# The gate ahead of the mixer by row blocks, twelve pairs of weight halves held, the norm's row folded into the scale

## The chip, the core and the metric

The kernel runs on one core of one Trainium2 chip. Its engines work side by side and wait for each other by semaphores: TensorE (PE in the rows) multiplies matrices and transposes, VectorE (DVE) does element-wise work, ScalarE (ACT) evaluates functions and copies, GpSimd (POOL) does some element-wise work, and SyncE (SP) issues the weight loads. Each engine takes its instructions in the order in which they stand in its queue. The metric is the time of one execution on the device in microseconds, of which the median over several runs counts.

## What is computed

The reference is a large block (a linear recurrence, attention, a mixture of 64 experts, a gate) followed by a second one (a mixer with window attention and a convolution). The change lies at the joint of the two:

```python
    ple_gate = jax.nn.sigmoid(rmsnorm(x, ln_ple[layer]) @ w_ple_gate[layer])
    x = x + (p[layer] @ w_ple_proj[layer]) * ple_gate
    return x
...
    sh, sc, gt = _modulation(c, w_mod[i], b_mod[i])
...
    h = _rmsnorm(x, pre_g[i]) * (1.0 + sc[:, None, :]) + sh[:, None, :]
...
    parts = _split_in(h @ w_in[i])
```

There are 256 rows (tokens) and 1024 columns. The gate is a 1024 by 1024 matrix multiplication, a sigmoid (made from a tanh) and a sum into `x`. Then `x` is normed by row, scaled by a row vector, shifted by another, and multiplied by `w_in_2` (10,240 columns).

## The kernel before

A row block `i` is 128 rows, and there are two; a column chunk `c` is 512 columns, and the gate has two. `x`, `acc` (the sum so far), `pp` (`p @ w_ple_proj`) and `x3g` (the normed `x`) lie with rows on the partitions. A matrix multiplication needs its left side with columns on the partitions, so `x3g` is transposed on TensorE, four 128x128 pieces into a PSUM bank (`transpose4`), and taken out of the bank as two halves, `hi` and `lo` (`hl_from_bank`): ScalarE writes `hi`, VectorE subtracts it for `lo`. The result, `h2`, holds 8 row groups `kt` of 128 columns, two halves and 256 tokens. Weights are halved in the same way (`split`): ScalarE casts `hi` and VectorE or GpSimd subtracts for `lo` (`sub_turn`: "v" is VectorE always, "vg" the two in turn). Each product is then three matmuls, 512 columns wide: hi by hi, lo by hi, hi by lo. Pairs of weight halves live in pools of four pairs: `spp`, `sp`, `sx`; `Held` gives two more. A pair's buffer comes free when its last matmul is done.

In the kernel before, the gate's chunk 0 goes through `gemm_nat` (both row blocks for each `kt`, 48 matmuls) and chunk 1 through `gemm_rows` (row block 0 over all eight `kt`, then row block 1). `take_gate` finishes each of the four blocks: tanh, two VectorE steps, the square sum of the norm, and for three of them the multiplication by the scale row (`mixer_gain`). `mixer_scale(i)` closes a block's norm, with the power on GpSimd (`rstd`), and multiplies by the norm's factor and adds the shift row. `mixer_columns(i)` transposes the block. Chunk 2 of `w_in_2` follows by `gemm_rows`: row block 0, the transposes of block 1, row block 1. `post_row` makes a row vector that is needed much later, with two matmuls in fp32. `row_of` made three such rows in the expert stage (expert group 13), among them the scale row and the shift row (`rows2`).

Then come chunks 3, 0, 1, 4 and 5 of `w_in_2` by `gemm_nat` (`qkv_lane`), with the pairs from `sp` alone and the subtractions by VectorE and GpSimd in turn. Woven into chunk 3 are the transposes of the keys of chunk 2 (`k_lane`, `stack_heads`): `take_rope` turns each block of chunk 2 with three kinds of VectorE steps into `kx`, `hi_lo` makes the two halves `kn` of it (a cast on ScalarE, a subtraction on GpSimd), and TensorE transposes these. `kx` has one buffer.

The order on each queue comes from a scheduler that takes what the code lists and estimates when things are ready; TensorE alone stands in the order of the code. `tc.issue_after` adds that one instruction stands behind another on the same engine.

## Time and profile before

| | us |
|---|---|
| median of 3 runs | 1130.07 |
| the three runs | 1130.07, 1131.84, 1127.13 |
| the profiled execution | 1129.72 |
| its span, first to last instruction | 1128.1 |
| TensorE busy in the span | 1031.7 (91%) |
| VectorE, ScalarE, GpSimd busy | 572.7, 424.3, 300.3 |

The span is what the trace shows; 1.6 us lie around it. The joint, from the gate's first matmul to the first matmul of chunk 3 of `w_in_2`, runs from 735.1 to 780.5 us of the span. In a timeline row the first number is the start, the second the length, and a bracket gives how long the engine stood idle before it and what ended that. Neighbouring matmuls overlap, so their pace is read from their starts and not from their lengths.

### The profile page before, as it was taken

How to read it: one execution, taken by the hardware profiler on the slowest of the kernel's cores; microseconds unless marked ns; L12 is line 12 of the kernel's file. 1: busy time of each engine (PE TensorE's matmuls, PEld its weight loads, DVE VectorE, ACT ScalarE, POOL GpSimd, SP SyncE). 2: the span in 40 equal slices, each digit the busy share in tenths (PEclk: the TensorE clock that was granted, in tenths of full speed). 3: DMA queues.
4: the chain of work that ended last, by engine and by line, in shares of the span. 5: the costliest groups of instructions: out<-in, count | busy, mean ns of one | idle time of the engine just before them, and what ended most of it. 6: DMA issues, size and time to landing. Idle time of an engine off the chain costs nothing.

```text
span 1128.1 us, 17631 instructions
## 1 busy us (share of the span) xinstructions
PE 1031.7 (91%) x6844; PEld 730.8 (65%) x6848; DVE 572.7 (51%) x1155; ACT 424.3 (38%) x875; POOL 300.3 (27%) x257
## 2 busy tenths in 40 slices
PE   8998899999999769999996788798999999999997
PEld 6886679985444134444442233176889989999996
DVE  6967896474333122321222232186847798752465
ACT  6766754550111030100110011164457646545553
POOL 2554474450000000000000000003553363554462
PEclk9998999999999889999999798899999999999999
DMA  8672468778999999999999999972554434345531
GB/s 348 250 281 78 158 244 291 302 279 318 419 421 419 422 419 420 421 421 422 421 421 419 420 422 420 420 285 75 187 201 164 141 128 139 127 155 184 185 113 38
DMA packets 47260, 321.49 MB, mean 285 GB/s; under 512 B 5762, under 2 KB 6274, under 8 KB 9411
## 3 DMA queue, kind: packets, MB, share of 16 engines
q1 hardware_dynamic: 47090, 320.04, 72.3%
q8 instruction: 56, 0.92, 0.3%
q14 instruction: 34, 0.27, 0.1%
q0 software_dynamic: 80, 0.26, 0.1%
HBM read 319.23 MB, written 1.05 MB: 284 GB/s over the span
## 4 chain that ended last, share of the span: by engine, by line
PE 63%; DMA 19%; DVE 11%; ACT 3%; issue 3%; POOL 1%; SPq 0%; DVEq 0%; POOLq 0%; ACTq 0%
DMA w<-in_w_dram 19%; PE mm L246 8%; PE mm L248 8%; PE mm L247 8%; PE mm L1256 5%; PE mm L1296 3%; PE mm L209 3%; PE mm L208 3%; PE mm L210 3%; PE ps L1239 3%; PE ps L1223 3%; PE mm L1130 2%; PE mm L970 2%; DVE lo L191 2%; PE ps L173 2%
## 5 line engine op out<-in xcount | busy, mean ns | idle before, releaser
L187 ACT CAST hi<-w 128x512 fp32r<-128x512 f32 (+2 forms) x340 | 205.6, 617 | 178.9 <-PE mm L247 125.5
L191 POOL TENSOR_TENSOR lo<-w,hi 128x512 fp32r<-128x512 f32 x144 | 198.3, 1379 | 229.3 <-ACT hi L187 221.4
L191 DVE TENSOR_TENSOR lo<-w,hi 128x512 fp32r<-128x512 f32 (+2 forms) x196 | 148.3, 766 | 115.5 <-ACT hi L187 105.6
L1256 PE MATMUL mm<-w,xe 128*32 128x512 f32 x1024 | 128.8, 640 | 29.8 <-DMA w<-in_w_dram 22.7
L246 PE MATMUL mm<-h,hi 128*128 128x256 f32 x448 | 129.5, 289 | 0.0
L248 PE MATMUL mm<-h,lo 128*128 128x256 f32 x448 | 126.7, 283 | 0.1
L247 PE MATMUL mm<-h,hi 128*128 128x256 f32 x448 | 126.6, 283 | 0.0
L1256 PEld LDWEIGHTS mm<-w,xe 128*32 128x32 f32 x1024 | 30.2, 114 | 115.8 <-issue 60.8
L1278 DVE SCALAR_TENSOR_TENSOR th<-th,mm 128x256 f32<-128x256 f32 x16 | 6.7, 421 | 180.3 <-ACT th L1277 180.3
L246 PEld LDWEIGHTS mm<-h,hi 128*128 128x128 f32 x448 | 85.6, 191 | 3.1 <-issue 3.1
L248 PEld LDWEIGHTS mm<-h,lo 128*128 128x128 f32 x448 | 85.7, 191 | 0.3 <-DVE lo L191 0.3
L247 PEld LDWEIGHTS mm<-h,hi 128*128 128x128 f32 x448 | 85.7, 191 | 0.0
L1296 PE MATMUL mm<-w,hE 128*32 128x512 f32 x512 | 64.3, 626 | 15.9 <-DMA w<-in_w_dram 11.4
L1277 ACT ACTIVATE th<-mm 128x256 f32<-128x256 f32 x16 | 6.1, 384 | 192.1 <-PE mm L1256 175.5
L1241 DVE TENSOR_TENSOR acc<-acc,ps 128x512 f32<-128x512 f32 x60 | 41.2, 687 | 65.3 <-PE ps L1239 65.2
L1351 POOL DMA_DIRECT2D tabs<-in_tabs_dram x1 | 0.7, 737 | 269.5 <-DMA w<-in_w_dram 269.5
L1223 PEld LDWEIGHTS ps<-G,x 128*128 128x128 f32 x512 | 60.9, 198 | 15.2 <-issue 13.5
L1239 PE MATMUL ps<-y,cT 128*128 128x512 f32 x128 | 61.6, 624 | 9.8 <-ACT y L1302 9.8
L248 PE MATMUL mm<-hT,lo 128*128 128x256 f32 x224 | 65.1, 291 | 2.6 <-DVE lo L191 2.6
L169 POOL TENSOR_TENSOR s<-s,half 128x1 f32<-128x1 f32 (+1 forms) x6 | 4.0, 668 | 237.4 <-DVE s L167 237.4
L246 PE MATMUL mm<-hT,hi 128*128 128x256 f32 x224 | 66.5, 297 | 0.0
L247 PE MATMUL mm<-hT,hi 128*128 128x256 f32 x224 | 64.7, 289 | 0.0
(474 smaller groups left out, 2145.2 us busy)
## 6 DMA issues: line engine op xcount, KB each, us to landing
w<-in_w_dram SPq DMA_DIRECT2D x192, 1024.0 KB, 19.8
w<-in_w_in_dram SPq DMA_DIRECT2D x66, 1024.0 KB, 5.0
w<-in_w_mod_dram SPq DMA_DIRECT2D x12, 1024.0 KB, 8.2
w<-in_w_out_dram SPq DMA_DIRECT2D x4, 1024.0 KB, 7.9
w<-in_w_ple_gate_dram SPq DMA_DIRECT2D x4, 1024.0 KB, 12.3
w<-in_w_out_conv_dram SPq DMA_DIRECT2D x4, 1024.0 KB, 4.7
w<-in_w_out_attn_dram SPq DMA_DIRECT2D x4, 1024.0 KB, 4.7
w<-in_w_o_dram SPq DMA_DIRECT2D x4, 1024.0 KB, 4.8
```

Source lines behind the costliest of these rows:

```text
L187: nc.scalar.copy(hi[:, :n], wt[:, off:off + n])
L191: last_sub[eng is G] = eng.tensor_sub(lo[:, :n], wt[:, off:off + n], hi[:, :n])
L208: mm(ps[m][:, :n], ah, wh, start=kt == 0, stop=False)
L209: mm(ps[m][:, :n], al, wh, start=False, stop=False)
L246: mm(o, hi[:, c:c + P], ah, start=kt == 0 and b % 2 == 0, stop=False)
L247: mm(o, hi[:, c:c + P], al, start=False, stop=False)
L248: mm(o, lo[:, c:c + P], ah, start=False, stop=kt == kts - 1 and b % 2 == 1)
L1223: mm(b[:, k * P:(k + 1) * P], x[:, i, kt * P:(kt + 1) * P], Gt[i].rearrange("p e s -> p (e s)"), start=i == 0, stop=i == 1)
L1239: mm(b, cT[:, i * P:(i + 1) * P], y[:, c * 512:(c + 1) * 512], start=True, stop=True)
L1241: V.tensor_add(acc[:, i, s_], (acc if q else x)[:, i, s_], b)
L1256: mm(ps[32 * j:32 * j + 32, :], xe[:, kt, 32 * j:32 * j + 32], wt[:, j * 512:(j + 1) * 512], start=kt == 0, stop=kt == KT - 1)
L1296: mm(ps[32 * j:32 * j + 32, :], hE[:, ft, 32 * j:32 * j + 32], wt[:, j * 512:(j + 1) * 512], start=ft == 0, stop=ft == 1)
```

## The change

The gate's two chunks go through one new function, `gemm_turns`. It multiplies row block 0 by both chunks first (with the first four `kt` of chunk 0 for row block 1 as well), holds the other twelve pairs of weight halves in `sp`, `sx` and `spp`, and multiplies row block 1 by them afterwards. `take_gate` is cut in two, the tanh and the rest (`gated`). The multiplication by the scale row is folded into `mixer_scale` (one instruction: `x` by the norm's factor by the scale row), so `mixer_gain` goes, and the row of the shift is no longer made in the expert stage. The shift is added instead where the transposed block leaves PSUM: there it is one number for each partition, and each of the eight 128x128 pieces of a block has a column of its own, so a block leaves in eight ScalarE and eight VectorE steps of 128 columns instead of two and two of 512. The halves of `w_in_2`'s chunk 2 (`halve`, two `kt` at a time) are put by hand between these steps, the transposes of row block 0 stand between the gate's last matmuls, and `post_row` moves behind the transposes of row block 1.

```diff
+    def gemm_turns(sps, actT, chunks, done):
...
+        for c in range(2):
+            for kt in range(KT):
+                hl[c, kt] = split(sps[c * 2 + kt // 4], wt[c][kt // 4], (kt % 4) * 512, 512)
+                terms(c, 0, kt)
+                if c == 0 and kt < 4:
+                    terms(c, 1, kt)
+                if kt % 2:
+                    yield
+        for c in range(2):
+            done(c, 0, ps[c, 0])
+        for c in range(2):
+            for kt in range(4 - 4 * c, KT):
+                terms(c, 1, kt)
+                if kt % 2:
+                    yield
+            done(c, 1, ps[c, 1])
...
-            row_of(gd, rows2[:, 0], gpre)
-            row_of(gd, rows2[:, 1], modT)
+            row_of(gd, rows2, gpre)
...
-            chain_[i].append(V.scalar_tensor_tensor(x3g[:, i, s_], x3g[:, i, s_], r, rows2[:, 1, s_],
-                                                    op0=ALU.mult, op1=ALU.add))
+            done = V.scalar_tensor_tensor(x3g[:, i, s_], x[:, i, s_], r, rows2[:, s_], op0=ALU.mult, op1=ALU.mult)
...
-            turned = hl_from_bank(h2, c * 4, i, b)
+            with then(*turned):
+                turned = []
+                for j in range(4):
+                    kt = c * 4 + j
+                    src, shift = b[:, j * P:(j + 1) * P], modT[:, kt, 0:1]
+                    hi = act(h2[:, kt, 0, t_], src, AF.Identity, bias=shift)
+                    lo = V.scalar_tensor_tensor(h2[:, kt, 1, t_], src, shift, h2[:, kt, 0, t_], op0=ALU.add, op1=ALU.subtract)
+                    turned = [hi, lo]
...
-    lane = gemm_nat(spp, pT, chunk("w_ple_gate", 0), 512, both(take_gate(0)))
+    lane = gemm_turns((spp, sp, sx, spp), pT, [chunk("w_ple_gate", c) for c in range(2)], take_gate)
...
+    def halve(kt):
+        hl2[kt] = split((ahead, sp, sx, spp)[kt // 2], wt2[kt // 4], (kt % 4) * 512, 512)
...
+    weave((some(lane, 3), 1))
+    with then(scaled, chain_[0]):
+        halve(2)
+        halve(3)
+    with then(last_sub[False]):
+        second = gated(0, 1)
     turned = mixer_columns(0)
...
+    weave((lane, 1))
+    with then(turned[1]):
+        halve(4)
+        halve(5)
+    with then(last_sub[False]):
+        third = gated(1, 1)
+    with then(third, chain_[1]):
+        halve(6)
+        halve(7)
+    with then(last_sub[False]):
         mixer_scale(1)
```

What this does to the queues stands at three places. First TensorE, where the transposes of row block 0 stand (`pT` is the gate's left side, `mm_6152` and `mm_5962` the bank of chunk 1, row block 1, L1414 is `post_row`, `mm_6209` and `mm_6237` chunk 2 of `w_in_2`). Before:

```order
L227 MATMUL mm_6152<-hi_6135,pT_5789 128x512
L228 MATMUL mm_6152<-lo_6136,pT_5789 128x512
L1414 MATMUL ps_6185<-gtp_6181,ones_84 128x512
L1414 MATMUL ps_6188<-gtp_6181,ones_84 128x512
L173 MATMUL ps_6191<-cst_68,x3g_5965 128x128 x4
L173 MATMUL ps_6198<-cst_68,x3g_5965 128x128 x4
L226 MATMUL mm_6209<-ahead_6184,h2_5962 128x512
```

And now:

```order
L267 MATMUL mm_5962<-lo_6079,pT_5781 128x512
L173 MATMUL ps_6174<-cst_68,x3g_5957 128x128 x4
L173 MATMUL ps_6187<-cst_68,x3g_5957 128x128 x4
L265 MATMUL mm_5962<-hi_6085,pT_5781 128x512
L266 MATMUL mm_5962<-hi_6085,pT_5781 128x512
L267 MATMUL mm_5962<-lo_6086,pT_5781 128x512
```

The transposes of row block 0 moved ahead of the gate's last twelve matmuls, which now stand between them and the first use of their result, and `post_row` no longer stands there.

Second VectorE, from the transposed block 0 on, with the engines that each instruction waits for (`h2` is the transposed block, `lo_6255` and `lo_6262`, now `lo_6225` and `lo_6229`, are the `lo` halves of the last two `kt` of chunk 2's weights). Before:

```order
L1361 SCALAR_TENSOR_TENSOR x_69<-tq_5781,acc_3211 128x512 [waits DVE_49]
L179 TENSOR_TENSOR h2_5962<-ps_6191,h2_5962 128x4x128 [waits Activation_49]
L179 TENSOR_TENSOR h2_5962<-ps_6198,h2_5962 128x4x128 [waits Activation_49]
L1369 TENSOR_TENSOR x3g_5965<-x_69,rows2_5620 128x512 [waits DVE_49]
L1373 TENSOR_TENSOR s3_5966<-s3_5966 128x1 [waits Activation_49]
L191 TENSOR_TENSOR lo_6255<-w_6207,hi_6254 128x512 [waits Activation_49]
L167 TENSOR_SCALAR s3_5966<-s3_5966 128x1 [waits DVE_49]
L191 TENSOR_TENSOR lo_6262<-w_6207,hi_6261 128x512 [waits Activation_49]
```

And now, from the last four pieces of the block on:

```order
L1427 SCALAR_TENSOR_TENSOR h2_5954<-ps_6187,modT_80,h2_5954 128x128 [waits Activation_49] x3
L191 TENSOR_TENSOR lo_6214<-w_6133,hi_6213 128x512 [waits DMAHW1_49]
L191 TENSOR_TENSOR lo_6218<-w_6133,hi_6217 128x512
L1394 SCALAR_TENSOR_TENSOR tq_5773<-tq_5773,pp_4813 128x512
L1395 SCALAR_TENSOR_TENSOR x_69<-tq_5773,acc_3211 128x512 [waits DVE_49]
L191 TENSOR_TENSOR lo_6225<-w_6133,hi_6224 128x512 [waits PE_49,Activation_49]
L191 TENSOR_TENSOR lo_6229<-w_6133,hi_6228 128x512 [waits PE_49,Activation_49]
```

The weight halves of the last four `kt` of chunk 2 now stand behind all eight pieces of block 0, and the last two of them also behind the gate's last block. On ScalarE, which makes `hi` of each piece (L1426), the same place reads so now (L1389 is a tanh, L1396 a square):

```order
L1426 ACTIVATE h2_5954<-ps_6174,modT_80 128x128 [waits PE_49]
L1426 ACTIVATE h2_5954<-ps_6174,modT_80 128x128 [waits DVE_49]
L1396 ACTIVATE tq_5773,s3_5958<-x_69 128x512 [waits DVE_49]
L1426 ACTIVATE h2_5954<-ps_6174,modT_80 128x128 [waits DVE_49]
L1389 ACTIVATE tq_5773<-mm_5962,s1_2578 128x512 [waits PE_49]
L1426 ACTIVATE h2_5954<-ps_6174,modT_80 128x128 [waits DVE_49]
L1426 ACTIVATE h2_5954<-ps_6187,modT_80 128x128
L1426 ACTIVATE h2_5954<-ps_6187,modT_80 128x128 [waits DVE_49] x3
L1396 ACTIVATE tq_5773,s3_5958<-x_69 128x512 [waits DVE_49]
L187 CAST hi_6224<-w_6133 128x512 [waits Activation_49]
```

Where two casts of 512 columns waited for TensorE alone before, each piece but the first of a bank now waits for VectorE, with a square and a tanh in between, and the cast for `kt` 6 stands behind the square of the gate's last block.

Third ScalarE in chunk 3, by name (`hi_6393`, `hi_6403` are the casts of `kt` 2 and 3 before, `hi_6405`, `hi_6415` now; `kn_6303` and `kn_6315` are the first keys, `kn_6339` and `kn_6351` the second). Before:

```order
L187 CAST hi_6393<-w_6359 128x512
L978 CAST kn_6303<-kx_6295 128x8x64
L187 CAST hi_6403<-w_6359 128x512
L187 CAST hi_6427<-w_6425 128x512
L187 CAST hi_6437<-w_6425 128x512
L978 CAST kn_6339<-kx_6331 128x8x64
L187 CAST hi_6447<-w_6425 128x512
L187 CAST hi_6457<-w_6425 128x512
```

And now:

```order
L187 CAST hi_6405<-w_6371 128x512
L187 CAST hi_6415<-w_6371 128x512
L187 CAST hi_6439<-w_6437 128x512
L1011 CAST kn_6315<-kx_6307 128x8x64
L187 CAST hi_6449<-w_6437 128x512
L187 CAST hi_6459<-w_6437 128x512
L187 CAST hi_6469<-w_6437 128x512
L1011 CAST kn_6351<-kx_6343 128x8x64
```

The cast of the first keys moved behind those of `kt` 3 and 4, that of the second keys behind those of `kt` 6 and 7. GpSimd follows. Before:

```order
L191 TENSOR_TENSOR lo_6372<-w_6359,hi_6371 128x512
L979 TENSOR_TENSOR kn_6303<-kx_6295,kn_6303 128x8x64
L191 TENSOR_TENSOR lo_6404<-w_6359,hi_6403 128x512
L191 TENSOR_TENSOR lo_6438<-w_6425,hi_6437 128x512
L979 TENSOR_TENSOR kn_6339<-kx_6331,kn_6339 128x8x64
L191 TENSOR_TENSOR lo_6458<-w_6425,hi_6457 128x512
```

And now:

```order
L191 TENSOR_TENSOR lo_6384<-w_6371,hi_6383 128x512
L191 TENSOR_TENSOR lo_6416<-w_6371,hi_6415 128x512
L1012 TENSOR_TENSOR kn_6315<-kx_6307,kn_6315 128x8x64
L191 TENSOR_TENSOR lo_6450<-w_6437,hi_6449 128x512
L191 TENSOR_TENSOR lo_6470<-w_6437,hi_6469 128x512
L1012 TENSOR_TENSOR kn_6351<-kx_6343,kn_6351 128x8x64
```

The first keys' subtraction moved behind that of `kt` 3, the second keys' behind that of `kt` 7.

## Rows read from the trace of the kernel before

**Rows 1.** The page: busy us, share of the span and instructions of each engine.

```profile
PE 1031.7 (91%) x6844; PEld 730.8 (65%) x6848; DVE 572.7 (51%) x1155; ACT 424.3 (38%) x875; POOL 300.3 (27%) x257
```

**Rows 2.** Windows, sum of 783 to 1128 us: length, busy time by engine.

```profile
sum 345.00, PE 334.95 PEld 311.26 DVE 225.37 ACT 181.90 POOL 165.56; mean PE 47.85 PEld 44.47 DVE 32.20 ACT 25.98 POOL 23.65
```

**Rows 3.** Timeline of TensorE from 735 to 781 us: start, length, operation, idle before.

```profile
735.09 0.80 PE L208 MATMUL mm<-hi,pT 128*128 128x512 f32 x1
...
739.53 0.48 PE L208 MATMUL mm<-hi,pT 128*128 128x512 f32 x1
...
745.65 0.50 PE L208 MATMUL mm<-hi,pT 128*128 128x512 f32 x1 [0.41 <-ACT hi L187]
...
751.56 0.39 PE L226 MATMUL mm<-hi,pT 128*128 128x512 f32 x1
...
759.88 1.88 PE L1414 MATMUL ps<-gtp,ones 128*128 128x512 f32 x4
763.70 1.29 PE L173 MATMUL ps<-cst,x3g 128*128 128x128 f32 x8 [1.94 <-DVE x3g L1377]
...
766.20 0.79 PE L227 MATMUL mm<-ahead,h 128*128 128x512 f32 x1 [0.70 <-DVE h L179]
...
773.10 1.03 PE L173 MATMUL ps<-cst,x3g 128*128 128x128 f32 x8
774.37 0.49 PE L226 MATMUL mm<-ahead,h 128*128 128x512 f32 x1 [0.24 <-ACT h L179]
...
780.49 0.40 PE L208 MATMUL mm<-hi,h 128*128 128x512 f32 x1
```

**Rows 4.** Windows of 1 us, with PEclk, the granted clock, after the five engines.

```profile
767.00:768.00 1.00, 1.00 (x3) 0.79 (x3) 1.00 (x5) 0.33 (x1) 0.00 (x0) 0.50 0.06 16
...
769.00:770.00 1.00, 1.00 (x5) 0.82 (x4) 0.88 (x2) 0.00 (x0) 0.09 (x1) 0.77 0.54 66
```

**Rows 5.** Timeline of TensorE in the expert stage, around the rows of `row_of` (L1195).

```profile
671.71 5.83 PE L1195 MATMUL ps<-gd,ones 128*128 128x512 f32 x12
...
683.03 1.06 PE L1256 MATMUL mm<-w,xe 128*32 128x512 f32 x8 [1.07 <-DMA w<-in_w_dram]
```

**Rows 6.** Timeline of VectorE at the joint.

```profile
746.67 5.51 DVE L191 TENSOR_TENSOR lo<-w,hi 128x512 fp32r<-128x512 f32 x9 [0.35 <-ACT hi L187]
...
760.31 0.69 DVE L1361 SCALAR_TENSOR_TENSOR x<-tq,acc 128x512 f32<-128x512 f32 x1
...
762.80 1.41 DVE L1377 SCALAR_TENSOR_TENSOR x3g<-x3g,s,rows 128x512 f32<-128x512 f32 x2 [0.67 <-POOL s L169]
```

**Rows 7.** Timeline of ScalarE at the joint.

```profile
740.29 6.35 ACT L187 CAST hi<-w 128x512 fp32r<-128x512 f32 x12
...
761.03 0.63 ACT L1362 ACTIVATE tq<-x 128x512 f32<-128x512 f32 x1 [1.48 <-DVE x L1361]
```

**Rows 8.** Groups by shape on ScalarE: count, busy us, mean ns of one, idle before.

```profile
L779 ACT ACTIVATE on<-ob 128x128 f32<-128x128 f32 x8 | 2.1, 270 | 0.7 <-PE ob L774 0.7
L450 ACT ACTIVATE cf<-ps,vec 128x128 f32<-128x128 f32 x6 | 1.7, 376 | 0.0
```

**Rows 9.** The same on VectorE.

```profile
L1460 DVE TENSOR_TENSOR rot<-mm,tabs 128x128 f32<-128x128 f32 x32 | 7.0, 276 | 0.0
L783 DVE SCALAR_TENSOR_TENSOR on<-ob,r,og 128x128 f32<-128x128 f32 x8 | 2.4, 346 | 2.1 <-POOL r L169 2.1
```

**Rows 10.** Timeline of ScalarE in chunk 3.

```profile
783.88 0.62 ACT L978 CAST kn<-kx 128x512 fp32r<-128x512 f32 x1
785.36 0.62 ACT L187 CAST hi<-w 128x512 fp32r<-128x512 f32 x1 [0.86 <-PE mm L209]
```

**Rows 11.** Timeline of GpSimd in chunk 3.

```profile
783.98 1.29 POOL L191 TENSOR_TENSOR lo<-w,hi 128x512 fp32r<-128x512 f32 x1 [1.65 <-ACT hi L187]
785.23 1.29 POOL L979 TENSOR_TENSOR kn<-kx,kn 128x512 fp32r<-128x512 f32 x1
```

**Rows 12.** Timeline of TensorE in chunk 3, the transposes of the second keys.

```profile
786.70 0.80 PE L985 MATMUL ps<-identr,kn 128*128 128x128 f32 x8
```

More of the change, by code (lines that the diff above doesn't have):

```diff
@@ L213, in gemm_nat, with gemm_rows @@
                 yield
-    def gemm_rows(sps, actT, halves, n, done):
-        wt = [wload(src, 4 * n) for src in halves]
-        hl = {}
+    def gemm_rows(sps, actT, halves, n, done, hl=None):
+        given = hl is not None
+        if not given:
+            wt = [wload(src, 4 * n) for src in halves]
+            hl = {}
         for m in range(NT):
@@ L220, in gemm_rows @@
             for kt in range(KT):
-                if m == 0:
+                if m == 0 and not given:
                     hl[kt] = split(sps[kt % len(sps)], wt[kt // 4], (kt % 4) * n, n)
@@ L251, in gemm_t, with terms @@
                 yield
+    def gemm_turns(sps, actT, chunks, done):
+        ps = {(c, m): bank("mm") for c in range(2) for m in range(NT)}
+        wt = [[wload(src) for src in halves] for halves in chunks]
+        hl = {}
+        def terms(c, m, kt):
+            wh, wl = hl[c, kt]
+            ah = actT[:, kt, 0, m * P:(m + 1) * P]
+            al = actT[:, kt, 1, m * P:(m + 1) * P]
+            mm(ps[c, m], ah, wh, start=kt == 0, stop=False)
+            mm(ps[c, m], al, wh, start=False, stop=False)
+            mm(ps[c, m], ah, wl, start=False, stop=kt == KT - 1)
+        for c in range(2):
[14 more added lines that the diff above has]
+            done(c, 1, ps[c, 1])
     class Held:
@@ L1317 @@
             gple = gd[:, :D]
[L1318 removed]
+            rows2 = md.tile([P, D], F32, name="rows2", tag="fT")
             row_of(gd, gple, vcol("ln_ple")[:, :, None])
[L1320 to L1321 removed]
+            row_of(gd, rows2, gpre)
         if q == NQ - 2:
@@ L1376, in mixer_scale, with then @@
             s_ = slice(c * 512, (c + 1) * 512)
-            chain_[i].append(V.scalar_tensor_tensor(x3g[:, i, s_], x3g[:, i, s_], r, rows2[:, 1, s_],
-                                                    op0=ALU.mult, op1=ALU.add))
+            done = V.scalar_tensor_tensor(x3g[:, i, s_], x[:, i, s_], r, rows2[:, s_], op0=ALU.mult, op1=ALU.mult)
+        return done
+    def then(*made):
+        order = ExitStack()
+        for m in made:
+            order.enter_context(tc.issue_after(m.ins))
+        return order
     def mixer_columns(i):
+        t_ = slice(i * P, (i + 1) * P)
+        turned = []
         for c in range(2):
@@ L1397 @@
     weave((some(lane, 1), 1))
-    chain_ = {}
     with tc.issue_after(seen[0].ins), tc.issue_after(seen[1].ins):
-        weave((lane, 1))
-        with tc.issue_after(last_sub[False].ins):
-            lane = gemm_rows((sp, sx), pT, chunk("w_ple_gate", 1), 512, take_gate(1))
-            weave((some(lane, 4), 1))
-        mixer_scale(0)
-        with tc.issue_after(chain_[0][0].ins), tc.issue_after(chain_[0][-1].ins):
-            weave((lane, 1))
-    dump("x3", x)
+        weave((some(lane, 7), 1))
+    with tc.issue_after(last_sub[False].ins), tc.issue_after(tanhs[1, 0].ins):
+        gated(0, 0)
+        first = gated(1, 0)
     gtp = ha.tile([P, D], F32, name="gtp")
@@ L1420 @@
                         modT[:, 16 + 4 * c:20 + 4 * c, 0:1].to_broadcast([P, 4, P]), op=ALU.mult)
[L1421 removed]
+    held, hl2 = {}, {}
     ahead = Held(w0.tile([P, 4, 512], F32R, name="ahead", tag="w"))
[L1423 to L1430 removed]
+    wt2 = [wload(src) for src in chunk("w_in_2", 2)]
+    def halve(kt):
+        hl2[kt] = split((ahead, sp, sx, spp)[kt // 2], wt2[kt // 4], (kt % 4) * 512, 512)
+    with then(first, tanhs[0, 0]):
+        halve(0)
+        halve(1)
+    with then(last_sub[False]):
+        scaled = mixer_scale(0)
+    weave((some(lane, 3), 1))
[4 more added lines that the diff above has]
+        second = gated(0, 1)
+    turned = mixer_columns(0)
+    weave((lane, 1))
[7 more added lines that the diff above has]
+        halve(7)
+    with then(last_sub[False]):
         mixer_scale(1)
[L1432 to L1433 removed]
+    dump("x3", x)
+    lane = gemm_rows(None, h2, None, 512, held.__setitem__, hl2)
+    weave((some(lane, 4), 1))
     turned = mixer_columns(1)
+    post_row(0)
+    post_row(1)
     spp_cm.__exit__(None, None, None)
```

32 lines of the change are left out of this document (9 added, 23 removed).

## The prediction

> **What bounds the kernel now.** I read the page first, then the windows, then one timeline per engine at the joint. TensorE is busy for 91% of the span [rows 1]. Behind the joint it is busy for 334.95 of 345.00 us [rows 2]: what TensorE loses or wins up to 783 us comes out at the end unchanged, and only TensorE's queue has to be followed. Around the joint it is another matter. From the gate's first matmul at 735.09 to the first of chunk 3 at 780.49 are 45.4 us [rows 3]. The pace of the wide matmuls is 36 from 751.56 to 759.88, 0.231 us each. The work of the stretch is 96 + 48 of these (33.3), three sets of eight transposes at 1.03 (3.1) and the post rows (1.9): 38.3 us. So 7.1 us are to be had there at most. They are seen in rows 3: a wait of 1.94 for VectorE's `x3g`, one of 0.70 for `h`, and smaller ones. Behind these waits the granted clock is 0.50, the level of 1.2 GHz, until it is back at 2.4 within the window that reads 0.77 [rows 4]: the 23 matmuls from 766.20 to 773.10 take 6.90 us where 23 x 0.231 = 5.3, so that stretch cost 1.6.
>
> **The change part by part.** I go through the queues in the printed order, with durations from rows, from the last point that is alike: `kt` 2 of chunk 0 begins at 739.53 [rows 3].
>
> *The row that goes.* `row_of` runs four of its twelve matmul records less, a third of 5.83, 1.9 us of TensorE. Its cover is the weight stream: at 683.03 TensorE waits for weights again [rows 5]. Price zero; without that cover it would be a gain of 1.9.
>
> *The gate.* VectorE's subtractions come every 0.60 us (9 in 5.51) [rows 6] and ScalarE's casts every 0.53 (12 in 6.35) [rows 7]. They stand in the order of use now, so neither is late for a `kt` that costs TensorE 3 x 0.231 = 0.69, and the wait of 0.41 at 745.65 goes [rows 3]. From 739.53 there are 48 matmuls to the end of block 0 (750.6) and 24 more before the transposes: 739.53 + 72 x 0.231 = 756.2. Is `x3g` there by then? Tanh from 750.9; VectorE's two steps, each about 0.70 with hand-over, to 753.0; the square as in rows 7 (0.6, and 0.2 to read its sum) to 753.8; behind two subtractions the sum and the scaling of the mean to 754.5; GpSimd's power, which cost VectorE a wait of 0.67; the scale, 1.41 for two [rows 6]: halves ready at 755.9 and 756.5. They are just in time. The transposes begin at 756.2 instead of 763.70: 7.5 us early. They and the twelve matmuls behind them end at 760.05.
>
> *The pieces.* This is the first unknown: a ScalarE step with a column, out of PSUM, 128x128, and the like on VectorE. The nearest rows are 376 ns (L450, with a column) and 270 (L779, without one) [rows 8], and 346 (L783) and 276 (L1460) [rows 9]. I take 376 and 346, which have the column and the bank as the new ones do. A hand-over is 0.03 us (VectorE ends at 761.00, ScalarE begins at 761.03) [rows 6, 7]. By the printed waits the engines take turns, so a pair costs 0.38 + 0.35 + 0.07 = 0.79, at the low ends 0.62. For block 0 the first `hi` is at 756.9, but VectorE has two subtractions and a gate step of 0.60 first, so `lo` is at 758.3; a gate step, a square and the last tanh (which waits for the twelve matmuls, 760.3) stand between the next; from 760.85 pairs follow each other and the last `lo` ends at 764.3.
>
> The Trainium skill speaks against this edit. Its page "PSUM — Partial Sum Buffer", section "PSUM bank collisions raise a hardware error", states that two engines may not use one bank in the same partitions at once, two reads included, so the pieces of a bank cannot leave on both engines together. The waits on VectorE that stand at ScalarE's pieces agree; no run shows the price yet. Were the pieces free of each other, the last `lo` would end about 1.5 us earlier (an estimate from the same rows), and the sum below would be 1134.5.
>
> *What is late next.* Row block 0 of chunk 2 starts at 760.05 instead of 765. Its first four `kt` run. Then TensorE needs `lo` of `kt` 4 at 763.3, and that stands behind the eight pieces on VectorE: it ends at 764.9, a wait of 1.6 (0.8 with the cheap pair). Behind it stand another subtraction and two gate steps to 766.8, then ScalarE's square to 767.5, and only then the cast for `kt` 6, to 768.1, where TensorE wants it at 765.9: a wait of 2.3. Two more subtractions, the norm's sum, the power and the scale make `x3g` of block 1 ready at 771.1; TensorE waits 0.4 to 1.4 for that. The second post row waits 0.75 for the copy of the first, whose bank it takes. In before, waits of 1.94 and 0.70 were followed by the half clock [rows 3, 4]; waits of 1.6 and 2.3 should be too, with most of it spent ahead of the wait for `x3g`: 0 to 0.9. Row block 1 starts at 775.0 to 775.8 (before 774.37) and chunk 3 at 780.5 to 781.4 (before 780.49) [rows 3]. All 7.5 us are given back; I take a loss of 0.4.
>
> *Chunk 3.* The diff does not touch it, the scheduler does. In before, the second keys were cast at 783.88 [rows 10], subtracted by GpSimd until 786.52 right behind one weight subtraction [rows 11], and transposed at 786.70 without a wait [rows 12]. Now their cast stands behind the casts of `kt` 6 and 7, and these need the buffers of `kt` 2 and 3: such a cast waits for TensorE (0.86 at 785.36 in rows 10). The matmuls of `kt` 3 stand directly ahead of the transposes on TensorE. So from the end of `kt` 3 there follow one after another, with TensorE idle, some 0.2 until the buffer is free, a cast of 0.62 [rows 10], the subtraction of `kt` 7 (1.25 to the next start) and that of the keys, 1.29 [rows 11]: 3.3 us. The first keys likewise stand behind the cast of `kt` 4, which needs the buffer of `kt` 0: with TensorE done with that buffer at 781.9, 0.52 to the next cast, 0.62 for it, 1.29 and the hand-overs make 784.4, and TensorE is there at 783.3: 1.1. The 3.3 us of idling should bring the half clock once more: 1.6, as above; 0 if it does not come, 3.2 if it stays twice as long. `kx` has one buffer, so the wait for the first keys does not shorten the second. Together 3.3 + 1.1 + 1.6 = 6.0.
>
> *Sum.* 0.4 + 6.0 = 6.4 on the profiled execution's 1129.72, which is 0.35 under the median: 1136.1. I write 1136.0.
>
> **Rivals.** (A) *The waits for the keys do not bind.* If the second keys' subtraction lands before TensorE comes, chunk 3 costs nothing: 1129.7 + 0.4 = 1130.1, not slower. It decides at 3.3 us: GpSimd must be done with the keys when `kt` 3 ends. For it speaks that in before the same step was just in time (786.52 against 786.70); against it, that the order of the casts and the buffer of `kt` 3 leave no way round. (B) *Block 0's pieces leave fast enough for chunk 2.* If the pairs cost so little that `lo` of `kt` 4 and the cast of `kt` 6 are there in time, 1.6 + 2.3 us of waits and the wait for `x3g` go, 5 us in all, the losses of chunk 3 stay: 1131. It would need a block in half the time of my pairs; the cheap pair of 0.62 saves only 0.8 for the first wait. (C) *A and B together*: 1130 - 5, 1125, faster. (D) *The half clock comes twice as often*, in row block 1 and over two stretches behind the keys, or the pairs cost a fifth more: 6.4 + 1.6 + 1 = 9, 1138.7. That the change doesn't do what it says is out: the transposes stand where the diff puts them.
>
> **How the numbers follow.** A measurement of this kernel can tell about 0.5%, 5.65 us, from no change, so "slower" begins at 1135.7, close to the forecast. My chances: forecast 0.68 (its own range 1133.5 to 1138), A 0.08, B 0.13, C 0.03, D 0.08. Of the forecast's 0.68 I put 0.50 above 1135.7, for it has more open ends there (the clock) than below (the cheap pair, no half clock), and 0.18 below. Slower: 0.50 + 0.08 = 0.58. Within 0.5%: 0.18 + 0.08 + 0.13 = 0.39. Faster: 0.03. The range takes the forecast's 0.68, half of D and two thirds of B: 1131 to 1139, 0.81.
>
> **What would show it.** Right: the transposes of block 0 near 756 without a wait; a wait of 1 to 2 us at `kt` 4 of chunk 2 for VectorE's `lo` and one of about 2 at `kt` 6 for ScalarE's `hi`; chunk 3's first matmul near 781; waits for GpSimd's `kn` of about 1 and 3 us ahead of the two sets of key transposes; granted clock 0.5 behind each pair of waits. Wrong in the gate's part: the transposes waiting for `x3g` well beyond 756. Wrong in the pieces: pairs under 0.6 us and chunk 3 beginning before 778. Wrong in chunk 3: the key transposes following the matmuls of `kt` 3 without a gap.

## The result, and the profile after

The changed kernel takes 1138.59 us (median of 8 runs, 1135.22 to 1140.93); the kernel before took 1131.05 beside it (8 runs). The ratio is 1.0073, 95% interval 1.0058 to 1.0088: 0.7% slower, a little beyond the 0.5% that the prediction takes as the least that can be told. The profiled execution took 1136.62, its span 1134.9, 6.8 more than before. TensorE has four matmul records fewer than in [rows 1] and is busy 3.2 us longer, so its work has become slower as well as later:

```profile
PE 1034.9 (91%) x6840; PEld 732.3 (65%) x6844; DVE 573.8 (51%) x1161; ACT 425.7 (38%) x885; POOL 301.5 (27%) x257
```

The timeline of TensorE, from the gate to chunk 3, answers to [rows 3] and [rows 12] (start, length, operation, idle before and what ended it):

```profile
735.02 0.80 PE L265 MATMUL mm<-hi,pT 128*128 128x512 f32 x1
...
756.24 1.12 PE L173 MATMUL ps<-cst,x3g 128*128 128x128 f32 x8
...
759.95 0.39 PE L228 MATMUL mm<-ahead,h 128*128 128x512 f32 x1
...
764.76 0.50 PE L230 MATMUL mm<-lo,h 128*128 128x512 f32 x1 [1.41 <-DVE lo L191]
...
767.95 0.50 PE L228 MATMUL mm<-hi,h 128*128 128x512 f32 x1 [1.98 <-ACT hi L187]
...
771.05 1.58 PE L173 MATMUL ps<-cst,x3g 128*128 128x128 f32 x8 [0.29 <-DVE x3g L1405]
...
774.16 1.13 PE L1453 MATMUL ps<-gtp,ones 128*128 128x512 f32 x2 [0.68 <-ACT gtp L1454]
...
780.65 0.39 PE L208 MATMUL mm<-hi,h 128*128 128x512 f32 x1
...
785.13 0.88 PE L1018 MATMUL ps<-identr,kn 128*128 128x128 f32 x8 [1.57 <-POOL kn L1012]
...
791.93 0.94 PE L1018 MATMUL ps<-identr,kn 128*128 128x128 f32 x8 [3.10 <-POOL kn L1012]
792.67 0.76 PE L208 MATMUL mm<-hi,h 128*128 128x512 f32 x1
...
796.12 0.39 PE L210 MATMUL mm<-lo,h 128*128 128x512 f32 x1
```

The transposes of block 0 stand 21.2 us behind the gate's first matmul, where they stood 28.6 behind it: 7.4 won, and no wait ahead of them. A part of this is order alone: twelve of the gate's matmuls (2.8 us) and the post rows (2.3, from 772.46 to 774.72, with a wait of 0.68) stood ahead of these transposes and now stand behind them. Row block 0 of chunk 2 begins 24.9 behind the gate's first matmul (759.95) instead of 29.9 (765.00 in before), 5.0 earlier. Of this nothing is left at chunk 3, which begins 45.63 behind the gate's first matmul instead of 45.41: the post rows take their time here now, 1.41 and 1.98 went into two waits of chunk 2, and the rest into smaller waits and into matmuls at the half clock. From chunk 3 to the end it is 354.29 instead of 347.56, 6.7 more: two waits for the keys' halves `kn`, 4.67 together, and the eight matmuls from 792.67 to 796.12, which take 3.45 where 8 x 0.23 = 1.84. Windows of 1 us show at which clock they ran; the number behind the five engines is the granted clock, 0.50 where it is 1.2 GHz:

```profile
769.00:770.00 1.00, 1.00 (x3) 0.82 (x3) 0.45 (x3) 0.00 (x0) 0.44 (x1) 0.50 0.00 0
...
793.00:794.00 1.00, 1.00 (x3) 0.80 (x3) 0.79 (x2) 0.00 (x0) 0.00 (x0) 0.50 1.04 442
```

All runs in one table. "Joint" is the stretch from the gate's first matmul to the first of chunk 3, "behind" the one from there to the last instruction, both from the profiled execution, so that differences ahead of the gate stay out; median and ratio come from all runs, and each ratio is to runs of the kernel before that were taken beside it.

| kernel | joint | behind | sum | median | ratio to before, 95% |
|---|---|---|---|---|---|
| before | 45.41 | 347.56 | 392.97 | 1131.05 | 1 |
| after | 45.63 | 354.29 | 399.92 | 1138.59 | 1.0073, 1.0058 to 1.0088 |
| after, again (e8) | 48.99 | 352.21 | 401.20 | 1140.24 | 1.0088, 1.0072 to 1.0105 |
| e1, casts first | 46.15 | 350.66 | 396.81 | 1138.45 | 1.0061, 1.0042 to 1.0080 |
| e2, keys in time | 45.77 | 350.37 | 396.14 | 1132.49 | 1.0022, 1.0010 to 1.0033 |
| e7, e2 with VectorE alone | 46.17 | 351.43 | 397.59 | 1133.97 | 1.0043, 1.0020 to 1.0066 |
| e3, whole banks | 41.85 | 347.55 | 389.39 | 1125.42 | 0.9966, 0.9951 to 0.9981 |
| e4, banks in turn | 44.70 | 347.79 | 392.50 | 1129.54 | 0.9988, 0.9977 to 1.0000 |
| e5, e3 with GpSimd | 41.52 | 347.57 | 389.10 | 1125.75 | 0.9964, 0.9952 to 0.9977 |
| e6, before with pieces | 43.50 | 353.92 | 397.41 | 1134.88 | 1.0032, 1.0019 to 1.0045 |
| e10, no half clock | 45.33 | 352.74 | 398.07 | 1133.38 | 1.0039, 1.0024 to 1.0054 |

### The profile page after: what moved, and what is told of

Same layout as the page of the kernel before. It is cut to its first block, busy times and chain, and to the rows that moved or that the text cites. A ratio compares the mean times of both kernels' runs of the same rounds, so it can differ in the third digit from the quotient of the medians.

```text
span 1134.9 us, 17638 instructions
## 1 busy us (share of the span) xinstructions
PE 1034.9 (91%) x6840; PEld 732.3 (65%) x6844; DVE 573.8 (51%) x1161; ACT 425.7 (38%) x885; POOL 301.5 (27%) x257
## 5 line engine op out<-in xcount | busy, mean ns | idle before, releaser
L1289 PE MATMUL mm<-w,xe 128*32 128x512 f32 x1024 | 132.6, 652 | 31.3 <-DMA w<-in_w_dram 23.8
L1289 PEld LDWEIGHTS mm<-w,xe 128*32 128x32 f32 x1024 | 29.9, 114 | 118.8 <-issue 58.3
L1329 PE MATMUL mm<-w,hE 128*32 128x512 f32 x512 | 61.9, 610 | 11.7 <-DMA w<-in_w_dram 6.9
L1256 PE MATMUL ps<-G,x 128*128 128x128 f32 x512 | 65.5, 288 | 0.5 <-DVE G L1248 0.5
L248 PE MATMUL mm<-hT,hi 128*128 128x256 f32 x224 | 65.8, 294 | 0.0
```

What stands on the lines that cost most here:

```text
L248: mm(o, hi[:, c:c + P], ah, start=kt == 0 and b % 2 == 0, stop=False)
L1256: mm(b[:, k * P:(k + 1) * P], x[:, i, kt * P:(kt + 1) * P], Gt[i].rearrange("p e s -> p (e s)"), start=i == 0, stop=i == 1)
L1289: mm(ps[32 * j:32 * j + 32, :], xe[:, kt, 32 * j:32 * j + 32], wt[:, j * 512:(j + 1) * 512], start=kt == 0, stop=kt == KT - 1)
L1329: mm(ps[32 * j:32 * j + 32, :], hE[:, ft, 32 * j:32 * j + 32], wt[:, j * 512:(j + 1) * 512], start=ft == 0, stop=ft == 1)
```

## The experiments

### The order of the keys' casts (e1)

`split` gets an order for two `kt` of chunk 3; `made` holds the keys' cast and subtraction.

```diff
-                    hi, lo = split(sp, wt, (pc * 2 + k) * n, n)
+                    with order(kt): hi, lo = split(sp, wt, (pc * 2 + k) * n, n)
...
+    kn, made, behind = {}, {}, {3: (0, 0), 6: (0, 1)}
...
+                made[c, i] = hi_lo(kn[c, i], d_, G)
...
+        yield from gemm_nat(sp, h2, chunk("w_in_2", 3), 512, both(take_rope(1, 1)), order=lambda kt: then(*made.get(behind.get(kt), ())))
```

> The changed kernel with one thing put back: in chunk 3 the keys' casts on ScalarE and their subtractions on GpSimd stand again where they stood before (first keys ahead of kt 3, second keys ahead of kt 6). VectorE's order is left alone. Theory A (the prediction's: the order of the casts makes the keys late): both waits for kn (1.57 and 3.10) go, and with them the half clock behind (1.6), 6.3 in all; against the kernel before 1.000 to 1.002. Theory B (VectorE's kx is late: its last step ends at 783.03, and the cast of the first keys already waits 0.48 for it): the first wait stays at 1.4 to 1.6, the second halves, since kx of the second row block is only done at 788.39, a cast of 0.62 and a subtraction of 1.27 follow, 790.4, and TensorE is there at 788.7: 1.7. With the half clock the gain is 1.4, without it 3.0; against the kernel before 1.004 to 1.006.

Timeline of TensorE, the two sets of key transposes:

```profile
785.12 0.87 PE L1018 MATMUL ps<-identr,kn 128*128 128x128 f32 x8 [0.54 <-POOL kn L1012]
...
790.84 0.86 PE L1018 MATMUL ps<-identr,kn 128*128 128x128 f32 x8 [2.03 <-POOL kn L1012]
```

Both waits shrink by about 1.0 and neither goes. By the profiled execution 3.1 us are won: these 2.1 and the half clock behind the second keys (1.5), less 0.5 in the joint. By the median it is nearly nothing (1.0061, near theory B). The five runs lie in two groups, 1134.1 twice, the profiled one among them, and 1138.5 to 1139.4 three times, so the size of the gain stays open. What the waits show does not: the prediction named a true chain, but behind it stands another. In the changed kernel ScalarE shows it: the cast of the first keys (L1011) waits for `kx` and not for a place in the queue.

```profile
783.12 0.62 ACT L1011 CAST kn<-kx 128x512 fp32r<-128x512 f32 x1 [0.48 <-DVE kx L1523]
...
788.69 0.62 ACT L187 CAST hi<-w 128x512 fp32r<-128x512 f32 x1 [0.74 <-PE mm L209]
789.22 0.61 ACT L1011 CAST kn<-kx 128x512 fp32r<-128x512 f32 x1
```

And VectorE shows why `kx` is late. It starts on it at 778.08, when the last piece of block 1 is out, 2.6 us ahead of chunk 3 (before, the last row below: 4.9 ahead of 780.49). Then two weight subtractions take 2.96, where two alone take 1.28, before the last step of `kx` (L1523) gets its turn:

```profile
778.08 0.68 DVE L1516 TENSOR_TENSOR kx<-mm,tabs 128x512 f32<-128x512 f32 x1
...
779.47 2.96 DVE L191 TENSOR_TENSOR lo<-w,hi 128x512 fp32r<-128x512 f32 x2
782.35 0.68 DVE L1523 TENSOR_TENSOR kx<-kx,rot 128x512 f32<-128x512 f32 x1
```

```profile
775.55 0.68 DVE L1455 TENSOR_TENSOR kx<-mm,tabs 128x512 f32<-128x512 f32 x1
```

GpSimd, in the same kernel, subtracts weight halves at the same time, and it too needs 2.99 for two where the prediction's row had 1.29 for one [rows 11]. For the second keys it shows the chain that the prediction described: a weight subtraction first, then that of the keys.

```profile
778.88 2.99 POOL L191 TENSOR_TENSOR lo<-w,hi 128x512 fp32r<-128x512 f32 x2 [8.77 <-ACT hi L187]
...
789.39 1.26 POOL L191 TENSOR_TENSOR lo<-w,hi 128x512 fp32r<-128x512 f32 x1 [3.07 <-ACT hi L187]
790.62 1.26 POOL L1012 TENSOR_TENSOR kn<-kx,kn 128x512 fp32r<-128x512 f32 x1
```

### VectorE's part of the keys put first as well (e2)

`made` holds the last step of `kx` too; the last number in `behind` says whether a weight half waits for that alone (1) or for the keys' two halves as well (3).

```diff
+    kn, made, behind = {}, {}, {0: (0, 0, 1), 2: (0, 0, 1), 3: (0, 0, 3), 6: (0, 1, 3)}
...
+                made[c, i] = turned_by, *hi_lo(kn[c, i], d_, G)
...
+                with then(*made[0, 1][:c + i < 1]): stack_heads(ko[:, c * 8:c * 8 + 8], i, kn[c, i])
```

> The kernel e1_casts_first with VectorE's order in chunk 3 changed as well: the last step of kx stands ahead of the weight subtractions of kt 0 and 2 (first keys) and ahead of the copies of the transposed first keys (second keys). Theory A and B both: first kx ready at 780.3 instead of 783.03, first keys at about 782.7, second at about 786.3, no wait for kn over 0.3, no half clock in chunk 3; the time falls by 6.0 to 6.6 against the changed kernel, 1.000 to 1.002 against the kernel before; all of the loss then was in chunk 3. Rival (the keys only take the place of weight halves, and VectorE and GpSimd slow each other): TensorE waits for lo of kt 0 to 3 instead, 2 us or more, and the time falls by under 4.

The first wait is gone and so is the half clock in chunk 3; a wait of 1.53 stays for the second keys:

```profile
789.59 0.88 PE L1018 MATMUL ps<-identr,kn 128*128 128x128 f32 x8 [1.53 <-POOL kn L1012]
```

The ratio falls to 1.0022, just above what both theories gave; by the profiled execution 3.8 us are won of the 6.0 or more. What holds the second keys is one VectorE step. Its timeline, and that of GpSimd behind it:

```profile
785.15 0.68 DVE L191 TENSOR_TENSOR lo<-w,hi 128x512 fp32r<-128x512 f32 x1
785.75 1.78 DVE L1523 TENSOR_TENSOR kx<-kx,rot 128x512 f32<-128x512 f32 x1
```

```profile
785.17 1.81 POOL L191 TENSOR_TENSOR lo<-w,hi 128x512 fp32r<-128x512 f32 x1 [0.19 <-ACT hi L187]
```

GpSimd starts at 785.17 beside VectorE's subtraction, which ends at 785.83, and ends at 786.98, 1.15 behind it. VectorE's next step starts at 785.75 and ends at 787.53, 0.55 behind GpSimd. Each waits for the other: of the 1.26 and 0.68 that these steps take alone, 1.15 and 0.55 come after the other engine's step has ended.

### Weight subtractions of chunk 3 on VectorE alone (e7)

```diff
-    sub_turn[1] = "vg"
+    sub_turn[1] = "v"
...
+            sub_turn[1] = "vg"; yield from gemm_nat(sp, h2, chunk("w_in_2", c), 512, both(take_rope(0, c)))
```

> The kernel e2_keys_in_time with all weight subtractions of chunk 3 on VectorE (GpSimd keeps those of the keys; from the next chunk on the two take turns again). In e2_keys_in_time the last steps of kx took 1.15 and 1.78 where others take 0.68, and GpSimd subtracted weight halves at the same time. Theory A (the two engines hinder each other): without GpSimd's weight subtractions these steps take 0.7, and the wait for the second keys falls from 1.53 to 0.4 to 0.9, although VectorE has three more subtractions of 0.60 in front of it. Rival (the long steps have another cause): steps of over 1 us stay, and the wait is 1.5 or more, up to 3.

The steps of `kx` take 0.69 and 0.68 now, as theory A said. But one of the four weight subtractions meets the keys' subtraction on GpSimd, and the four take 3.59 instead of 2.5 (VectorE, then GpSimd):

```profile
778.00 3.59 DVE L191 TENSOR_TENSOR lo<-w,hi 128x512 fp32r<-128x512 f32 x4
```

```profile
778.90 1.54 POOL L1012 TENSOR_TENSOR kn<-kx,kn 128x512 fp32r<-128x512 f32 x1 [11.48 <-ACT kn L1011]
```

The second wait became 2.00 instead of 1.53, with the half clock behind it: the second keys come 8.4 us behind chunk 3's first matmul, where they came 8.3 behind it in e2, since the meeting moved to another step and VectorE's queue is longer, and TensorE is there earlier. Theory A held for the long steps and failed for the wait.

### The gate by row blocks without the pieces (e3)

```diff
-            row_of(gd, rows2, gpre)
+            [row_of(gd, rows2[:, k], col) for k, col in enumerate((gpre, modT))]
...
+        return V.tensor_mul(x3g[:, i, s_], x[:, i, s_], rows2[:, 0, s_])
...
+            done = V.scalar_tensor_tensor(x3g[:, i, s_], x3g[:, i, s_], r, rows2[:, 1, s_], op0=ALU.mult, op1=ALU.add)
...
+                turned = hl_from_bank(h2, c * 4, i, b)
```

> The changed kernel with the shift row back: two rows are made in the expert stage again, VectorE multiplies by the scale row behind each gate block and adds the shift row in the norm's step, and a transposed block leaves its two banks in two steps of 512 columns on each engine instead of eight pieces. The gate by row blocks stays. Theory A (the pieces are what gives the gate's gain back): the transposes of block 0 stand at 756.2 to 757, the wait at kt 4 (1.41) goes, that at kt 6 (1.98) falls to about 0.4, the transposes of block 1 come near 768 with a wait of about 1.3, chunk 3 begins near 777 instead of 780.65; its keys are then in time as before, so the end is 9 to 10 us earlier than in the changed kernel, 0.996 to 0.999 against the kernel before. Rival (VectorE's load holds chunk 2, whatever the pieces): with the four multiplications by the scale row back, chunk 3 begins within 0.7 of 780.65 and only the keys' waits can change; 1.001 or more.

```profile
762.53 0.51 PE L228 MATMUL mm<-hi,h 128*128 128x512 f32 x1 [0.26 <-ACT hi L187]
...
765.63 1.29 PE L173 MATMUL ps<-cst,x3g 128*128 128x128 f32 x8 [1.17 <-DVE x3g L1405]
...
776.91 0.79 PE L1018 MATMUL ps<-identr,kn 128*128 128x128 f32 x8
```

Theory A, and a little more than it gave (10.5 us against the changed kernel, not 9 to 10): the wait at `kt` 4 is gone, that at `kt` 6 is 0.26, the joint is 3.8 shorter than in the changed kernel, the keys are in time without any edit of theirs (the scheduler has their casts ahead of the later weight halves again), and this version is a little faster than both kernels, 0.9966. The gate by row blocks, with the order of the steps that goes with it, is worth 3.6 us (389.39 against 392.97); what the change lost, it lost with the folding that makes the pieces, although that spares VectorE four multiplications.

### The pieces without the gate by row blocks (e6)

```diff
-            row_of(gd, rows2[:, 1], modT)
...
-            chain_[i].append(V.scalar_tensor_tensor(x3g[:, i, s_], x3g[:, i, s_], r, rows2[:, 1, s_],
-                                                    op0=ALU.mult, op1=ALU.add))
+            chain_[i].append(V.tensor_scalar(x3g[:, i, s_], x3g[:, i, s_], r, None,
+                                             op0=ALU.mult))
...
-            turned = hl_from_bank(h2, c * 4, i, b)
+            for j in range(4):
+                kt, src, shift, t_ = c * 4 + j, b[:, j * P:(j + 1) * P], modT[:, c * 4 + j, 0:1], slice(i * P, (i + 1) * P)
+                hi = act(h2[:, kt, 0, t_], src, AF.Identity, bias=shift)
+                turned = hi, V.scalar_tensor_tensor(h2[:, kt, 1, t_], src, shift, h2[:, kt, 0, t_], op0=ALU.add, op1=ALU.subtract)
```

> The kernel before with one part of the change alone: the row of the shift goes, the shift is added by column in sixteen pieces of 128 columns. The gate keeps its two chunks one after the other. Theory A (the pieces make the losses, in chunk 2 by taking turns and in chunk 3 because the keys' rotation stands behind them on VectorE and the scheduler puts the keys' casts behind kt 6 and 7 there too): the stretch from the gate's first matmul to chunk 3 stays within 1 us of the 45.4 of before, since TensorE uses a piece at about the pace at which pairs come (0.79 against 0.69), and chunk 3 has one or two waits for kn, 3 us or more in all, with the half clock behind; 1.003 to 1.005 against the kernel before. Rival (the losses come from the gate by row blocks, or need both parts): no wait for kn over 0.5, 0.998 to 1.001.

```profile
783.42 0.89 PE L985 MATMUL ps<-identr,kn 128*128 128x128 f32 x8 [1.11 <-POOL kn L979]
...
790.22 0.95 PE L985 MATMUL ps<-identr,kn 128*128 128x128 f32 x8 [3.10 <-POOL kn L979]
```

The same two waits, in a kernel whose gate was not touched: 6.4 us behind the joint. The joint itself got 1.9 shorter, where theory A allowed 1; in this execution the granted clock stays at 1.00 there. In the changed kernel's first execution and in e6, where the pieces are taken bank by bank, VectorE starts on `kx` 2.6 and 3.0 us ahead of chunk 3, in before, e3 and e4 4.9 to 6.0 ahead; only the former wait for keys. The casts of the keys differ in the same way: behind later weight halves in the former, ahead of them in the latter.

### The two banks in turn (e4)

```diff
+        for kt in (0, 4, 1, 5, 2, 6, 3, 7):
             with then(*turned):
-                turned = []
-                for j in range(4):
-                    kt = c * 4 + j
+                for j in (kt % 4,):
+                    b = banks[kt // 4]
```

> The changed kernel with the sixteen pieces in another order: the two banks of a block in turn (piece 0 of the first bank, piece 0 of the second, piece 1 of the first, and so on). Theory A (ScalarE waits for VectorE only within a bank): the two engines work side by side, a pair costs about 0.4 instead of 0.79, the last lo of block 0 ends near 762.5 instead of 764.1, the wait at kt 4 goes, that at kt 6 stays near 2 (its cast stands behind the gate's last block), and chunk 3 begins 0 to 1 us earlier than 780.65. In this kernel the keys' casts stand ahead of kt 3 and kt 6 again, so chunk 3 may gain what e1 or e2 gain. Rival (the engines take turns for another reason, or reading two banks at once slows each piece): pairs of 0.75 or more, last lo at 764 or later, wait at kt 4 of 1.3 or more.

ScalarE's pieces, first in the changed kernel (block 0), one each 0.79, with the casts of `kt` 6 and 7 far behind:

```profile
762.57 0.37 ACT L1426 ACTIVATE h<-ps,modT 128x128 fp32r<-128x128 f32 x1 [0.42 <-DVE h L1427]
763.35 0.37 ACT L1426 ACTIVATE h<-ps,modT 128x128 fp32r<-128x128 f32 x1 [0.42 <-DVE h L1427]
...
767.30 1.12 ACT L187 CAST hi<-w 128x512 fp32r<-128x512 f32 x2
```

then in e4 (block 1), two each 0.79:

```profile
770.53 0.62 ACT L1426 ACTIVATE h<-ps,modT 128x128 fp32r<-128x128 f32 x2 [0.16 <-DVE h L1427]
771.32 0.37 ACT L1426 ACTIVATE h<-ps,modT 128x128 fp32r<-128x128 f32 x1 [0.16 <-DVE h L1427]
```

So the engines took turns by bank, and a pair's price halves when the other bank is there to work on. The Trainium skill's page "PSUM — Partial Sum Buffer", section "PSUM bank collisions raise a hardware error", says that two engines may not use one bank in the same partitions at the same time; the two paces agree with it. The wait at `kt` 4 is gone, the one at `kt` 6 is not, and the one for the copy of the first post row has grown from 0.68:

```profile
755.25 1.12 PE L173 MATMUL ps<-cst,x3g 128*128 128x128 f32 x8
...
765.38 0.50 PE L228 MATMUL mm<-hi,h 128*128 128x512 f32 x1 [2.00 <-ACT hi L187]
...
772.22 1.13 PE L1453 MATMUL ps<-gtp,ones 128*128 128x512 f32 x2 [1.65 <-ACT gtp L1454]
```

The last `lo` of block 0, counted from the transposes, ends 1.6 earlier (VectorE's last piece, first in the changed kernel, then in e4):

```profile
763.75 0.35 DVE L1427 SCALAR_TENSOR_TENSOR h<-ps,modT,h 128x128 fp32r<-128x128 f32 x1 [0.43 <-ACT h L1426]
```

```profile
761.19 0.35 DVE L1427 SCALAR_TENSOR_TENSOR h<-ps,modT,h 128x128 fp32r<-128x128 f32 x1 [0.18 <-ACT h L1426]
```

The whole chain behind it moved with it: `kt` 6 begins 10.13 behind the transposes instead of 11.71. TensorE's wait there is as long as before because TensorE, spared the wait at `kt` 4, comes as much earlier. Then the post rows give 1.0 back. The joint is 0.9 shorter, the keys are in time (VectorE starts on `kx` 5.8 ahead of chunk 3), and the time is that of before, 0.9988. The same pieces in another order thus give back 7.4 us (399.92 against 392.50), nearly all of the loss; the order of the keys' casts, which the scheduler chose anew, is part of that.

### More of it on GpSimd (e5)

```diff
+        sub_turn[1] = "g"
+        halve(6)
+        halve(7)
+    sub_turn[1] = "v"
     with then(last_sub[False]):
         third = gated(1, 1)
-    with then(third, chain_[1]):
-        halve(6)
-        halve(7)
-    with then(last_sub[False]):
         mixer_scale(1)
```

> The kernel e3_whole_banks with the weight halves of kt 6 and 7 of chunk 2 made earlier and elsewhere: their casts stand right behind the transposed block 0 on ScalarE instead of behind the gate's last block, and GpSimd, which is idle there, subtracts them. In e3_whole_banks VectorE closes block 1's norm at 763.72 behind these two subtractions, and TensorE waits 0.26 at kt 6 and 1.17 at the transposes of block 1. Theory A (VectorE's queue sets the transposes of block 1): they come 1.1 to 1.5 earlier, both waits fall under 0.3 each, chunk 3 begins 1.2 to 1.7 earlier counted from the gate's first matmul; 0.9945 to 0.996 against the kernel before. Rival (VectorE and GpSimd slow each other, as the steps of 1.2 to 1.8 beside GpSimd's subtractions in e2_keys_in_time suggest): VectorE's steps between block 0 and the norm are stretched by 1 us or more in all, and the gain is under 0.5.

VectorE and GpSimd, and the wait that was to go:

```profile
758.93 2.67 DVE L191 TENSOR_TENSOR lo<-w,hi 128x512 fp32r<-128x512 f32 x2
```

```profile
758.05 3.00 POOL L191 TENSOR_TENSOR lo<-w,hi 128x512 fp32r<-128x512 f32 x2 [3.49 <-ACT hi L187]
```

```profile
766.71 1.29 PE L173 MATMUL ps<-cst,x3g 128*128 128x128 f32 x8 [1.59 <-DVE x3g L1405]
```

The rival: VectorE was spared 1.2 us of subtractions and paid 1.4 more for two others (2.67 against 1.28). The wait for `x3g` is longer, the joint 0.3 shorter, the ratio that of e3.

### The changed kernel again, and without the half clock (e8, e10)

> The changed kernel as it is, once more. Its profiled execution was 6.9 above that of before, the medians lie 7.5 apart. Theory A (which stretches run at the half clock differs between executions, and in some the half clock behind the waits lasts longer or comes one stretch more): the waits at kt 4, kt 6 and for the keys return within 0.2 of 1.41, 1.98, 1.57 and 3.10, while the stretch from the gate's first matmul to the last instruction differs by a multiple of about 1.6 from 399.9. Rival (the rest lies in the expert stage, whose length differs between executions of any kernel): that stretch is 399.9 within 0.4 again, and only the time ahead of the gate differs, by up to 3.

The waits at `kt` 4, `kt` 6 and for the second keys came back as 1.41, 1.99 and 3.10. But the half clock lay elsewhere: it held from 770 to 780 (one of its windows below) and did not come behind the keys. Block 1's transposes, the post rows and the first six matmuls of row block 1 ran in it.

```profile
774.00:775.00 1.00, 1.00 (x2) 0.00 (x0) 0.07 (x1) 0.00 (x0) 0.00 (x0) 0.50 0.00 0
```

The joint became 48.99 instead of 45.63, the stretch behind 352.21 instead of 354.29. The first keys' wait became 0.99, since `kx` had more time: VectorE was done with it at 785.53, and their cast stands right behind that of `kt` 4, which waits for TensorE:

```profile
785.70 0.62 ACT L187 CAST hi<-w 128x512 fp32r<-128x512 f32 x1 [3.35 <-PE mm L209]
786.22 0.61 ACT L1011 CAST kn<-kx 128x512 fp32r<-128x512 f32 x1
```

Theory A in kind; the difference is 1.3, not a multiple of 1.6. The next kernel takes the half clock away and leaves the waits.

```diff
+    for n in (0, 0, 5, 7): keep_warm(n, "ob") or next(lane)
...
+                keep_warm((0, 0, 6, 12)[2 - 2 * c + i] * (1 - c), "ob") or stack_heads(ko[:, c * 8:c * 8 + 8], i, kn[c, i])
```

> The changed kernel with idle matmuls in four of TensorE's waits: 5 ahead of kt 4 and 7 ahead of kt 6 of chunk 2 (waits of 1.41 and 1.98), 6 ahead of the first and 12 ahead of the second keys' transposes (1.57 and 3.10). Each takes 0.23 us, so they fit into the waits; all that other engines do stays. Two profiled executions of the changed kernel had the half clock in different places: one from 768.7 to 772.1 and again behind the second keys, 399.9 from the gate's first matmul to the end, the other from 769.9 to 780.2 and not behind the keys, 401.2. Theory A (the waits are followed by the half clock, and its share is 1.6 to 3.5 us and lands differently from one execution to the next): TensorE stays at 2.4 GHz from 735 on, the waits themselves end at the same times, and from the gate's first matmul to the end it is 397.5 to 398.5; 1.004 to 1.006 against the kernel before, 2 to 4 us under the changed kernel. Rival (the half clock costs nothing here, since TensorE waits at its end anyway): no gain over 0.5.

One window over the whole stretch, with the granted clock at 1.00, and TensorE around the second keys:

```profile
735.00:800.00 65.00, 61.49 (x277) 44.74 (x278) 44.69 (x90) 33.61 (x71) 13.18 (x12) 1.00 0.45 165
```

```profile
786.37 2.80 PE L158 MATMUL ob<-warm 128*128 128x512 bf16 x12
789.63 0.89 PE L1018 MATMUL ps<-identr,kn 128*128 128x128 f32 x8 [0.46 <-POOL kn L1012]
```

Theory A: 398.07, and 1.0039 against 1.0073 and 1.0088 for the kernel without these matmuls. What the half clock costs the changed kernel is 1.9 and 3.1 us in its two profiled executions and 3.8 and 5.5 by the two ratios, each give or take about 2.4 by their intervals. The rest of the loss, 4.4 by the ratio and 5.1 by the profile, is the waits; the kernel before, against which it is counted, has its own stretch at the half clock (1.6, from [rows 3] and [rows 4]).

## Why the prediction was right or wrong

**The gate: right.** Transposes of block 0 forecast at 756.2 without a wait, found at 756.24 without one. That the row that went gave nothing is not contradicted: e3 makes it again and its gate begins at 732.3, but over all runs, with the row and without it, the gate begins between 732.3 and 735.9, and a gain of 1.9 would not stand out there.

**The pieces: right.** A pair at 0.79, found 0.79; last `lo` forecast at 764.3, found 764.10. The estimate that the last `lo` would come 1.5 us earlier if the pieces were free of each other was right too: counted from the transposes it came 1.6 earlier in e4. What that is worth was not: 1.5 was taken off the sum, and e4 took 7.4 off. Of these 0.9 lie in the joint and 6.5 behind it, since the keys came in time and the half clock stayed away.

**Chunk 2: right in every link, a little high.** 1.6, 2.3, 0.4 to 1.4 and 0.75 were forecast for `kt` 4, `kt` 6, `x3g` and the second post row; found 1.41, 1.98, 0.29 and 0.68. Chunk 3 at 780.5 to 781.4, found 780.65. "All 7.5 us are given back; I take a loss of 0.4" came out as 0.2.

**Chunk 3: the size right, the cause half right.** 3.3 + 1.1 + 1.6 = 6.0 was forecast, 3.10 + 1.57 + 1.6 and 0.4 of small parts were found, 6.7. The chain for the second keys stood there link by link, and that for the first keys, "stand behind the cast of `kt` 4", stood alone in e8, where it gave 0.99 for the forecast 1.1. The step that failed is that nothing else holds the keys: VectorE's part in `kx` stands in no term of the sum. In the first execution `kx` came 0.48 later than ScalarE was free for it, which makes the first wait 1.57 instead of 1.1, and e1, which lifted the order of the casts, still waited 0.54 and 2.03: right behind the forecast's chain stood another, nearly as late. VectorE was late because its turn at `kx` comes behind block 1's pieces and because its weight subtractions met GpSimd's: two took 2.96 instead of 1.28. The prices for these steps in the prediction, 0.60 [rows 6] and 1.29 [rows 11], are those of engines that leave each other alone; side by side both took 1.5 a step.

**The half clock: the mis-sized term.** 0 to 0.9 in the joint and 1.6 in chunk 3 were forecast, 1.6 to 2.5 in all. e10 puts it at 1.9 and 3.1 in two executions and at 3.8 and 5.5 by the ratios. The profiled execution, 6.9 above that of before and 0.5 from the forecast's 6.4, had it cheap; by the medians the kernel is 7.5 above, by the ratio 8.2. With 4 in place of its 1.6 the sum would have been 1138.5, an estimate. The prediction held one execution's clock for the kernel's. Why the ratios give more than the two profiles is not shown. A part can be chance, with intervals this wide; another part is on record in the mean granted clock of each run: in e8 the profiled execution has 0.963, and the other three, with 0.955 to 0.957, took 1.7 to 2.8 us longer. In the changed kernel's own eight runs clock and time do not go together like this.

**The rivals.** A fell: the waits bound. B's price was wrong. It said that pieces in half the time would save 5 us in chunk 2; e4 had pairs at half the price, its last `lo` came 1.6 earlier, and the joint gained 0.9: two subtractions, two gate steps, a square and the cast still stand between the last piece and `kt` 6. e3, in which the gate's last block no longer waits behind the pieces on VectorE, had 3.8 of B's gain. D was near in size; neither profiled execution has the clock quite as D says, but e10 bears out the first of its two reasons, a half clock that costs more, while the pairs cost what was forecast.

## What to carry to other kernels

A step cut into pieces is paid for on the queue behind it: sixteen pieces a block in place of four whole steps cost 4.4 and 10.5 us (e6 against before, the changed kernel against e3). In both VectorE came later to its next work, `kx`, by 1.9 and 3.4 us counted from chunk 3, and the scheduler moved the keys' casts back as well; how much each of the two costs, e1 and e2 show only in part. Two engines that take turns at one bank can be given two banks: in e4 that halved a pair's price. When a reordering and a folding come in one change, run each alone: here the one was worth 3.6 us, and the other hid it. And ask of a late operand for the second-latest chain too, before undoing the first.
